# Four recurrent and attention layers on one core: x transposed once, the first norm on transposed tiles with a broadcast row, the residual copy from the same transposes

## The chip, the cores and the metric

The kernel runs on one core of a Trainium2 chip. Its engines work side by side, each on its own instruction queue in order: TensorE (PE, matmuls and transposes into PSUM; PEld is its weight load), VectorE (DVE), ScalarE (ACT), GpSimd (POOL) and SyncE (SP), whose queue issues the DMAs here. They wait for each other through semaphores. The metric is the device time of one execution in microseconds (us); for the kernel before, the median of three runs is 2333.66 us.

## The reference, cut to what matters

The input x has 1024 rows (positions) of 1024 channels, in f32. Two blocks of two layers each follow one another: a gated linear recurrence, attention with a shared low-rank cache, a layer with differential attention and a state-space scan, and sliding-window attention. Each layer adds its result to x. The change is in the first norm and the first lines of the first layer:

```python
def rms_norm(x, g):
    xf = x.astype(jnp.float32)
    y = xf * lax.rsqrt(jnp.mean(xf * xf, axis=-1, keepdims=True) + EPS)
    return (y * g.astype(jnp.float32)).astype(x.dtype)

def rglru_layer(x, norm_g, w_in, conv_w, ...):
    h = rms_norm(x, norm_g)
    u = h @ w_in
    xb, gate = u[..., :D_RNN], u[..., D_RNN:]
    xb = causal_depthwise_conv(xb, conv_w, conv_b)
    ...
    y = hs.astype(x.dtype) * jax.nn.silu(gate)
    return y @ w_out

x = x + rglru_layer(x, norm_a[layer], ...)
```

So every row of x needs one factor, the reciprocal root of its mean square, every channel one gain, and x itself is needed again for the residual.

## The kernel before, in words

Matmuls contract over the partitions, so activations are kept transposed: channels on the 128 partitions, positions along the free axis, in two halves of 512 positions. An f32 product is made of three matmuls in the fast format f32r: each operand is split into a rounded part and a remainder (`split`: ScalarE casts, VectorE subtracts), and high times high, high times low and low times high are added in PSUM (`mm3`, called by `proj`). The normalized input of a layer is the set of tiles `hT`: for each half, high and low, eight channel blocks in four tiles.

`start_phase` makes the first `hT`. It loads x in eight tiles `xt` of 128 positions, each in two halves, and the gains once for all 128 partitions (`gb`). For each tile ScalarE squares and sums the rows (into `xn`, whose content is not used), VectorE and POOL make the factor `r`, VectorE multiplies by factor and gain (`xn`), TensorE transposes (`tp0`, shown as `tp_140` and so on), and the result is split straight from PSUM. Then, with a lower priority (`LATE`), it transposes the raw `xt` again (`tpx`), copies to SBUF (`xe`, on ScalarE or VectorE, whichever is free) and stores to the DRAM scratch `xT_d`, from which the first layer's `out_proj` later reads the residual. `load_cols` loads small gains as rows, transposes them (`cps`) and keeps them as columns.

`layer_A` then projects with `w_in` in five pairs of 128 output channels. The weights come through `load_w`: loads `raw`, splits `whi` and `wlo`. In the first pair (`pr == 0`) the matmuls are 256 positions wide, so that they can begin when a quarter of x is ready; in the other pairs they are 512 wide. Each needs all eight channel blocks.

The order of the instructions on each engine is not the order of the code. Every call is recorded as an `Op` with a price in nanoseconds (`price`), its predecessors and its buffers, and `schedule` plays the whole program through in a list schedule: whenever an engine is free it takes the ready operation with the lowest priority number (its place in the code plus a bias). What comes out is emitted in `emit`, so all instructions carry line 429. A price that changes can therefore move instructions in every stage. Buffers come from pools with a limit for each name; a tile is given out when the plan finds one free. The stages after the start are, in order of time: the recurrence (to about 290 us), its output projection (to 390), the second layer's norm and projections, its attention, its output projection (to 935), the third layer, the fourth, and the last projection with the final norm.

Of the kernel before, what the change touches and what calls it, by code (L numbers as in the profile page):

```python
# [10 lines left out]
F32 = mybir.dt.float32  # L11
F32R = mybir.dt.float32r
AF = mybir.ActivationFunctionType
ALU = mybir.AluOpType
# [4 lines left out]
D = 1024  # L19
HALF = 512  # L20
# [153 lines left out]
class Program:  # L174
# [78 lines left out]
    def price(self, op):  # L253
# [40 lines left out]
    def schedule(self):  # L294
# [40 lines left out]
        while left:  # L335
            progress = False
            for e in engines:
# [95 lines left out]
def tile_kernel(ctx: ExitStack, tc: tile.TileContext, A, cc, out, stages="AMEO", dump=False):  # L433
# [38 lines left out]
    def begin(**tags):  # L472
        E.begin({k: v for k, v in tags.items()})
        E.cur.update(gtag)
# [62 lines left out]
    def split(hi, lo, src):  # L537
        splits((hi, lo, src))
# [168 lines left out]
    def start_phase(wsrc):  # L707
        begin(hT=("c4", 17), xt=("c4", 6), gb=("c4", 4), xn=("c4", 2), xe=("c2", 7), rows=("c2", 2), r1=("xs", 12),
              tp0=("ps", 2), tpx=("ps", 2), cps=("ps", 1))
        ht = new_hT()  # L710
        E.sync.dma_start(out=ident, in_=cc[:, C_ID:C_ID + 128])
        gb = T("gb", [128, D])
        xts, w = [], None
        for t in range(8):
            xt = T("xt", [128, D])
            for q in range(2):
                E.sync.dma_start(out=xt[:, q * 512:(q + 1) * 512], in_=A["x"][0, t * 128:(t + 1) * 128, q * 512:(q + 1) * 512])
            xts.append(xt)
            if t == 0:
                E.sync.dma_start(out=gb, in_=A["norm_a"][0].partition_broadcast(128))  # L720
            if t == WPOS:
                w = load_w(*wsrc)
        for t in range(8):
            xt, h, o = xts[t], t // 4, (t % 4) * 128
# [3 lines left out]
            E.vector.tensor_scalar(out=r[:, 1:2], in0=r[:, 0:1], scalar1=1.0 / D, scalar2=1e-6, op0=ALU.mult, op1=ALU.add)  # L728
            E.gpsimd.tensor_tensor(out=r[:, 2:3], in0=r[:, 1:2], in1=mhalf[:, 0:1], op=ALU.pow)
            for q in range(2):  # L730
                qs = slice(q * 512, (q + 1) * 512)
                E.vector.scalar_tensor_tensor(out=xn[:, qs], in0=xt[:, qs], scalar=r[:, 2:3], in1=gb[:, qs], op0=ALU.mult, op1=ALU.mult)
                tp = T("tp0", [128, 4, 128])
                for j in range(4):
                    E.tensor.transpose(tp[:, j], xn[:, (q * 4 + j) * 128:(q * 4 + j + 1) * 128], ident)
                splits(*[[ht[h][n][q * 2 + j][:, :, o:o + 128] for n in range(2)] + [tp[:, 2 * j:2 * j + 2]] for j in range(2)])
        E.bias += LATE
        for t in range(8):
            for q in range(2):
                tp = T("tpx", [128, 4, 128])  # L740
                for j in range(4):
                    E.tensor.transpose(tp[:, j], xts[t][:, (q * 4 + j) * 128:(q * 4 + j + 1) * 128], ident)
                xe = T("xe", [128, 4, 128])
                E.scalar.copy(xe, tp)
                E.alt("vector", "tensor_copy", (), dict(out=xe, in_=tp))
                E.sync.dma_start(out=xT_d[q * 4:(q + 1) * 4, :, t * 128:(t + 1) * 128].rearrange("k p s -> p k s"), in_=xe)
        E.bias -= LATE
        load_cols(0, [("norm_a", R(A["norm_a"][0])), ("conv_w", R2(A["conv_w"][0])), ("conv_b", R(A["conv_b"][0])),
                      ("b_rg", R(A["b_rg"][0])), ("b_ig", R(A["b_ig"][0])), ("lam", R(A["lru_lambda"][0])),
# [67 lines left out]
    def layer_A(ht, nxt):  # L817
# [14 lines left out]
        for pr in range(5):  # L832
# [12 lines left out]
            if pr == 0:  # L845
                for h in range(2):
                    pss = [T("mm", [128, HALF]) for b in range(2)]
                    for t in range(2):
                        ts = slice(t * 256, (t + 1) * 256)
                        for b in range(2):  # L850
                            proj(pss[b][:, ts], wx, b * 128, lambda k: tuple(x[k // 2][:, k % 2, ts] for x in ht[h]), 8)
                    for b in range(2):
                        E.scalar.copy(xss[b][:, 3 + h * HALF:3 + (h + 1) * HALF], pss[b])
# [688 lines left out]
```

## Time and profile before

| | |
|---|---|
| median of three runs | 2333.66 us (2333.2 to 2335.78) |
| the profiled execution: time, span | 2334.89 us, 2333.1 us |
| PE busy in the span | 2302.8 us (99%), 12233 instructions |
| PEld, DVE, ACT, POOL busy | 1943.9, 1575.0, 1273.2, 97.1 us |
| mean granted TensorE clock | 0.998 of full speed |
| DMA | 191.60 MB, 82 GB/s on the mean |

The span runs from the first to the last instruction. A busy time is the sum over an engine's instructions, overlaps taken once. A matmul's own duration holds its way through the array, so the pace of matmuls that follow one another is read from how many fit into a stretch, not from their mean. A wait is an idle time of an engine together with what ended it. The granted clock is the share of TensorE's full speed of 2.4 GHz that the chip allowed; 0.50 is its lower level, 1.2 GHz.

### The profile page before, as it was taken

How to read it: one execution, taken by the hardware profiler on the slowest of the kernel's cores; microseconds unless marked ns; L12 is line 12 of the kernel's file. 1: busy time of each engine (PE TensorE's matmuls, PEld its weight loads, DVE VectorE, ACT ScalarE, POOL GpSimd, SP SyncE). 2: the span in 40 equal slices, each digit the busy share in tenths (PEclk: the TensorE clock that was granted, in tenths of full speed). 3: DMA queues.
4: the chain of work that ended last, by engine and by line, in shares of the span. 5: the costliest groups of instructions: out<-in, count | busy, mean ns of one | idle time of the engine just before them, and what ended most of it. 6: DMA issues, size and time to landing. Idle time of an engine off the chain costs nothing.

```text
span 2333.1 us, 33127 instructions
## 1 busy us (share of the span) xinstructions
PE 2302.8 (99%) x12233; PEld 1943.9 (83%) x12233; DVE 1575.0 (68%) x3646; ACT 1273.2 (55%) x2653; POOL 97.1 (4%) x133
## 2 busy tenths in 40 slices
PE   8999999999999999999999999999999999999998
PEld 7888788778999888889898988888878888888877
DVE  6666735553777865876776758787776336787775
ACT  6766723332666653565656656585542125777751
POOL 0000001110000001000000000000001000000000
PEclk9999999999999999999999999999999999999999
DMA  6211322222112512312112111343243113111341
GB/s 191 84 41 37 113 95 90 73 84 82 48 55 60 194 55 67 109 42 59 38 44 58 44 55 48 106 121 116 69 176 138 55 55 108 50 55 46 112 141 73
DMA packets 171189, 191.60 MB, mean 82 GB/s; under 512 B 18294, under 2 KB 129170, under 8 KB 171026
## 3 DMA queue, kind: packets, MB, share of 16 engines
q1 hardware_dynamic: 171025, 189.48, 25.7%
q8 instruction: 96, 1.57, 0.3%
q14 instruction: 68, 0.55, 0.1%
HBM read 145.30 MB, written 42.04 MB: 80 GB/s over the span
## 4 chain that ended last, share of the span: by engine, by line
PE 96%; DVE 2%; ACT 1%; DMA 1%; issue 0%; SPq 0%; POOL 0%; DVEq 0%; POOLq 0%; ACTq 0%
PE mm L429 53%; PE ops L429 19%; PE sc L429 8%; PE ov L429 6%; PE tps L429 4%; PE yo L429 1%; PE tp L429 1%; PE mg L429 1%; PE nps L429 1%; PE aux L429 1%; DMA gb<-in_norm_a_dram 0%; PE ftp L429 0%; ACT s L429 0%; DVE xn L429 0%; PE tpx L429 0%
## 5 line engine op out<-in xcount | busy, mean ns | idle before, releaser
L429 PE MATMUL mm<-hT,whi 128*128 128x512 f32 (+1 forms) x3136 | 1002.9, 394 | 0.5 <-ACT whi L429 0.5
L429 PEld LDWEIGHTS mm<-hT,whi 128*128 128x128 f32 x3136 | 577.4, 188 | 120.9 <-issue 1.7
L429 PE MATMUL mm<-hT,wlo 128*128 128x512 f32 (+1 forms) x1568 | 616.2, 394 | 0.0
L429 PEld LDWEIGHTS mm<-hT,wlo 128*128 128x128 f32 x1568 | 294.8, 188 | 58.8 <-issue 0.5
L429 ACT ACTIVATE s<-s,st 128x257 f32<-128x257 f32 (+9 forms) x446 | 284.7, 656 | 92.9 <-DVE st L429 89.9
L429 DVE TENSOR_TENSOR wlo<-raw,whi 128x512 fp32r<-128x512 f32 (+4 forms) x316 | 200.4, 656 | 73.9 <-ACT whi L429 33.8
L429 ACT CAST whi<-raw 128x512 fp32r<-128x512 f32 (+4 forms) x316 | 176.1, 587 | 71.7 <-DVE wlo L429 44.9
L429 PE MATMUL ops<-yl,whi 128*128 128x512 f32 x544 | 214.3, 395 | 0.3 <-DVE yl L429 0.3
L429 PE MATMUL ops<-yh,whi 128*128 128x512 f32 x544 | 213.8, 395 | 0.0
L429 PE MATMUL ops<-yh,wlo 128*128 128x512 f32 x544 | 213.3, 394 | 0.0
L429 DVE TENSOR_TENSOR pl<-tps,ph 128x512 fp32r<-128x512 f32 (+2 forms) x284 | 142.9, 535 | 79.8 <-ACT ph L429 77.8
L429 DVE TENSOR_TENSOR xr<-ops,xr 128x512 f32<-128x512 f32 x96 | 65.9, 690 | 187.9 <-PE ops L429 187.9
L429 DVE CUSTOM_DVE_ANT_0 s<-sc,bt 128x256 f32<-128x256 f32 (+3 forms) x320 | 149.9, 491 | 36.5 <-PE sc L429 35.0
L429 ACT CAST ph<-tps 128x512 fp32r<-128x512 f32 (+2 forms) x284 | 121.3, 469 | 97.2 <-PE tps L429 95.4
L429 PE MATMUL ov<-ph,v 128*128 128x256 f32 (+2 forms) x700 | 159.6, 286 | 0.8 <-ACT ph L429 0.7
L429 ACT ACTIVATE sq<-xr 128x512 f32<-128x512 f32 x58 | 36.7, 632 | 208.7 <-DVE xr L429 208.6
L429 PE MATMUL tps<-ident,s 128*128 128x128 f32 x816 | 137.5, 273 | 0.2 <-DVE pl L429 0.2
L429 PEld LDWEIGHTS ov<-ph,v 128*128 128x128 f32 x700 | 118.1, 189 | 11.6 <-ACT ph L429 3.2
L429 PEld LDWEIGHTS ops<-yl,whi 128*128 128x128 f32 x544 | 102.1, 188 | 24.6 <-DVE yl L429 1.1
L429 PEld LDWEIGHTS ops<-yh,whi 128*128 128x128 f32 x544 | 102.0, 188 | 24.1 <-issue 0.3
L429 PEld LDWEIGHTS ops<-yh,wlo 128*128 128x128 f32 x544 | 102.2, 188 | 23.6
L429 PE MATMUL ov<-pl,v 128*128 128x256 f32 (+1 forms) x380 | 117.5, 309 | 0.5 <-DVE pl L429 0.5
(295 smaller groups left out, 3884.6 us busy)
## 6 DMA issues: line engine op xcount, KB each, us to landing
raw<-in_w_in_a_dram SPq DMA_DIRECT2D x72, 512.0 KB
raw<-in_w_out_a_dram SPq DMA_DIRECT2D x24, 512.0 KB
xr<-xT_d SPq DMA_DIRECT2D x24, 512.0 KB
yl<-yA_d SPq DMA_DIRECT2D x48, 256.0 KB
raw<-in_w_in_c_dram SPq DMA_DIRECT2D x18, 512.0 KB
xT_d<-xr SPq DMA_DIRECT2D x32, 256.0 KB
yA_d<-y SPq DMA_DIRECT2D x32, 256.0 KB
csb<-cs_d SPq DMA_DIRECT2D x16, 512.0 KB
```

The lines of the kernel that those rows point to most:

```text
L429: getattr(getattr(nc, op.eng), op.method)(*[conv(a) for a in op.args], **{k: conv(v) for k, v in op.kwargs.items()})
```

## The change

x is loaded in whole tiles of 128 positions. The gains come as a column (`cols["norm_a"]`, by an early `load_cols`) instead of a row spread over all partitions. For each half of 512 positions, four tiles are squared, the four columns of factors are made at once, spread on a diagonal (`dg`), and one plain f32 matmul with a matrix of ones puts the row of 512 factors on all partitions (`bc0`, in PSUM). Raw x is transposed once (`tp0`); `xe` is the copy in SBUF, one channel block by 512 positions. From `xe` VectorE makes `xn` with the gain column and the factor row, and `split` makes `hT`; the same `xe` is stored to `xT_d`. The `tpx` transposes and the bias `LATE` there are gone. In `layer_A` the first pair's matmuls are 512 wide and half by half. In `price` the matmul prices change, and in `schedule` the assumed DMA rate goes from 200 to 300 bytes per nanosecond.

```diff
         elif op.method == "matmul":
             fast = any(x.base.dt == F32R for x in reads)
             if fast:
-                op.cost = max(107, n / 2.4) + 2.5
+                op.cost = max(109, n * 0.449 + 2.5)
             elif n == 1:
-                op.cost = 150
+                op.cost = 224
             else:
-                op.cost = n / 0.6 * (0.55 if v.shape[0] == 64 else 1) + 2.5
+                op.cost = max(224, n / 0.6) * (0.5 if v.shape[0] == 64 else 1) + 2.5
...
-                    dma_free = max(dma_free, now + 2000) + op.nbytes / 200.0
+                    dma_free = max(dma_free, now + 2000) + op.nbytes / 300.0
...
     def start_phase(wsrc):
-        begin(hT=("c4", 17), xt=("c4", 6), gb=("c4", 4), xn=("c4", 2), xe=("c2", 7), rows=("c2", 2), r1=("xs", 12),
-              tp0=("ps", 2), tpx=("ps", 2), cps=("ps", 1))
+        begin(hT=("c4", 17), xt=("c4", 8), sqx=("c4", 2), xe=("c2", 7), xn=("c2", 3), rows=("c2", 2), dg=("c2", 1), r1=("xs", 12),
+              tp0=("ps", 3), bc0=("ps", 2), cps=("ps", 1))
...
+        load_cols(2, [("norm_a", R(A["norm_a"][0]))])
         xts, w = [], None
         for t in range(8):
             xt = T("xt", [128, D])
-            for q in range(2):
-                E.sync.dma_start(out=xt[:, q * 512:(q + 1) * 512], in_=A["x"][0, t * 128:(t + 1) * 128, q * 512:(q + 1) * 512])
+            E.sync.dma_start(out=xt, in_=A["x"][0, t * 128:(t + 1) * 128])
             xts.append(xt)
-            if t == 0:
-                E.sync.dma_start(out=gb, in_=A["norm_a"][0].partition_broadcast(128))
...
-        for t in range(8):
-            xt, h, o = xts[t], t // 4, (t % 4) * 128
-            r = T("r1", [128, 4])
-            xn = T("xn", [128, D])
-            E.scalar.activation(xn, xt, AF.Square, accum_out=r[:, 0:1])
...
-        E.bias += LATE
-        for t in range(8):
-            for q in range(2):
-                tp = T("tpx", [128, 4, 128])
...
+        gain = cols["norm_a"]
+        for h in range(2):
+            r = T("r1", [128, 8])
+            for j in range(4):
+                junk = T("sqx", [128, D])
+                E.scalar.activation(junk, xts[h * 4 + j], AF.Square, accum_out=r[:, j:j + 1])
+            E.vector.tensor_scalar(out=r[:, 0:4], in0=r[:, 0:4], scalar1=1.0 / D, scalar2=1e-6, op0=ALU.mult, op1=ALU.add)
+            E.gpsimd.tensor_tensor(out=r[:, 4:8], in0=r[:, 0:4], in1=mhalf[:, 0:4], op=ALU.pow)
+            dg = T("dg", [128, 4, 128])
+            E.vector.tensor_tensor(out=dg, in0=ident.unsqueeze(1).to_broadcast([128, 4, 128]),
+                                   in1=r[:, 4:8].unsqueeze(2).to_broadcast([128, 4, 128]), op=ALU.mult)
+            bc = T("bc0", [128, 512])
+            E.tensor.matmul(bc, lhsT=ones_r.bitcast(F32), rhs=dg.rearrange("p a b -> p (a b)"), start=True, stop=True)
+            for k in range(8):
                 tp = T("tp0", [128, 4, 128])
                 for j in range(4):
+                    E.tensor.transpose(tp[:, j], xts[h * 4 + j][:, k * 128:(k + 1) * 128], ident)
+                xe = T("xe", [128, 512])
+                E.scalar.copy(xe, tp.rearrange("p a b -> p (a b)"))
+                E.alt("vector", "tensor_copy", (), dict(out=xe, in_=tp.rearrange("p a b -> p (a b)")))
+                xn = T("xn", [128, 512])
+                E.vector.scalar_tensor_tensor(out=xn, in0=xe, scalar=gain[:, k:k + 1], in1=bc, op0=ALU.mult, op1=ALU.mult)
+                split(ht[h][0][k // 2][:, k % 2], ht[h][1][k // 2][:, k % 2], xn)
+                E.sync.dma_start(out=xT_d[k, :, hs(h)], in_=xe)
...
-            for b, h in ([] if pr == 0 else [(0, 0), (0, 1), (1, 0), (1, 1)]):
+            for b, h in ([(0, 0), (1, 0), (0, 1), (1, 1)] if pr == 0 else [(0, 0), (0, 1), (1, 0), (1, 1)]):
                 ps = T("mm", [128, HALF])
                 proj(ps, wx, b * 128, hrhs(ht, h), 8)
```

TensorE's queue before, from its first instruction on: `tpx` are transposes of raw x, `tp_140` and so on those of normalized x, `mm` the first projection.

```order
L429 MATMUL tpx<-ident,xt 128x128 x8
L429 MATMUL tp_140<-ident,xn 128x128 x4
L429 MATMUL tpx<-ident,xt 128x128 x3
L429 MATMUL tp_152<-ident,xn 128x128 x4
L429 MATMUL tpx<-ident,xt 128x128 x13
L429 MATMUL tp_215<-ident,xn 128x128 x4
L429 MATMUL tpx<-ident,xt 128x128 x3
L429 MATMUL tp_231<-ident,xn 128x128 x4
L429 MATMUL tpx<-ident,xt 128x128 x5
L429 MATMUL tp_257<-ident,xn 128x128 x4
L429 MATMUL tp_274<-ident,xn 128x128 x4
L429 MATMUL mm<-hT,whi 128x256 x4
```

And now, from the last transpose of the third channel block on, with the factor row `bc_217` and the first projection matmuls:

```order
L429 MATMUL tp_123<-ident,xt 128x128
L429 MATMUL tp_161<-ident,xt 128x128 x4
L429 MATMUL tp_168<-ident,xt 128x128 x4
L429 MATMUL tp_179<-ident,xt 128x128 x4
L429 MATMUL tp_188<-ident,xt 128x128 x4
L429 MATMUL tp_198<-ident,xt 128x128 x4
L429 MATMUL bc_217<-dg,ones_r 128x512
L429 MATMUL tp_223<-ident,xt 128x128
L429 MATMUL tp_225<-ident,xt 128x128
L429 MATMUL tp_223<-ident,xt 128x128
L429 MATMUL tp_225<-ident,xt 128x128
L429 MATMUL mm<-hT,whi 128x512 x2
```

The first projection matmul stood behind 24 transposes of four tiles of x and 32 of the copy; it now stands behind all 32 transposes of a half and the factor row, and the copy has no transposes of its own.

VectorE's queue now, from the first evacuation on (`r_115` the mean squares of four tiles, `cols_77` the gain column, `wlo` the weights' remainder):

```order
L429 COPY xe<-tp_117 128x512
L429 COPY xe<-tp_119 128x512
L429 TENSOR_SCALAR r_115<-r_115 128x4
L429 COPY xe<-tp_161 128x512
L429 COPY xe<-tp_168 128x512
L429 TENSOR_TENSOR wlo<-raw,whi 128x512 x2
L429 TENSOR_TENSOR dg<-ident,r_115 128x512
L429 TENSOR_TENSOR wlo<-raw,whi 128x512 x2
L429 SCALAR_TENSOR_TENSOR xn<-xe,cols_77,bc_217 128x512 x3
L429 TENSOR_TENSOR hT<-xn,hT 128x512
L429 SCALAR_TENSOR_TENSOR xn<-xe,cols_77,bc_217 128x512
L429 TENSOR_TENSOR hT<-xn,hT 128x512 x2
```

Before, the first `xn` was VectorE's third instruction after one evacuation; now four evacuations and four weight remainders stand ahead of it.

SP's queue of DMAs now, in the middle of the start (`rows` are the small gains, `raw` the next weights):

```order
L429 DMA rows<-in_conv_b_a_dram 12x128
L429 DMA xT_d<-xe 128x512 x7
L429 DMA rows<-in_ssd_norm_a_dram 8x128
L429 DMA rows<-in_subln_a_dram 1x128
L429 DMA rows<-in_norm_c_dram 8x128
L429 DMA rows<-in_b_in_c_dram 18x128
L429 DMA raw<-in_w_in_a_dram 128x4x256 x2
L429 DMA xT_d<-xe 128x512 x7
```

Seven stores of the copy have moved ahead of the last four gain loads and of the next weights; before, the first store was issued behind all gain loads.

## Rows read from the trace of the kernel before

**Rows 1.** The page's line of TensorE: busy us, share of the span, instructions.
```profile
PE 2302.8 (99%) x12233; PEld 1943.9 (83%) x12233; DVE 1575.0 (68%) x3646; ACT 1273.2 (55%) x2653; POOL 97.1 (4%) x133
```

**Rows 2.** Busy us by stretch: length, PE, PEld, DVE, ACT, POOL, PEclk, DMA share, GB/s.
```profile
0.00:60.00 60.00, 48.44 (x344) 45.39 (x345) 41.12 (x102) 37.22 (x81) 4.89 (x16) 0.97 0.64 194
60.00:2230.00 2170.00, 2161.19 (x11486) 1824.11 (x11485) 1473.50 (x3430) 1201.64 (x2494) 87.79 (x109) 1.00 0.25 79
2230.00:2333.10 103.10, 93.17 (x406) 74.35 (x405) 60.42 (x116) 34.30 (x80) 4.41 (x8) 0.98 0.20 72
```

**Rows 3.** TensorE's waits, first stretch and middle: us in total, times, longest.
```profile
PE tpx L429 <- DMA xt<-in_x_dram: 4.0, 1, 4.0
...
PE nps L429 <- ACT dh L429: 3.3, 3, 1.6
PE mm L429 <- ACT krh L429: 2.1, 2, 1.4
...
PE ov L429 <- DVE pl L429: 0.5, 1, 0.5
```

**Rows 4.** The chain that ended last, from the start: start us, us, what.
```profile
2.12 7.06 DMA gb<-in_norm_a_dram
...
11.95 0.85 PE tp L429 x4
...
39.03 0.44 PE tp L429 x4
...
42.73 8.05 PE mm L429 x68
...
65.70 3.72 PE mm L429 x16
```

**Rows 5.** Timeline of TensorE at plain f32 products: start us, us, what.
```profile
1516.57 1.72 PE L429 MATMUL tp<-xdd,BN 128*128 128x128 f32 x14
1518.05 0.48 PE L429 MATMUL mm<-hT,whi 128*128 128x512 f32 x1
```

**Rows 6.** Busy us of short stretches at the start, columns as in rows 2.
```profile
4.00:7.00 3.00, 1.94 (x8) 1.57 (x8) 0.85 (x2) 1.63 (x3) 0.00 (x0) 1.00 0.82 182
9.00:13.00 4.00, 2.78 (x13) 2.81 (x14) 2.17 (x4) 0.65 (x2) 0.00 (x0) 1.00 1.07 385
14.84:16.95 2.11, 0.01 (x1) 0.00 (x1) 1.44 (x5) 2.11 (x6) 0.55 (x1) 1.00 0.84 298
17.40:20.80 3.40, 3.40 (x18) 3.33 (x16) 2.45 (x8) 2.20 (x6) 0.55 (x1) 0.50 0.58 186
```

**Rows 7.** Groups by form: busy us, mean ns | idle before.
```profile
L429 ACT ACTIVATE xn<-xt 128x1024 f32<-128x1024 f32 x8 | 8.6, 1074 | 0.0
...
L429 DVE COPY xe<-tpx 128x512 f32<-128x512 f32 x2 | 1.4, 692 | 6.1 <-PE tpx L429 6.1
...
L429 POOL TENSOR_TENSOR r<-r,mhalf 128x4 f32<-128x4 f32 x32 | 37.0, 1158 | 817.3 <-DVE r L429 804.8 <-DMA yB_d<-yb 6.3 <-DVE sk L429 3.4
...
L429 DVE TENSOR_TENSOR wlo<-raw,whi 128x512 fp32r<-128x512 f32 x8 | 5.1, 682 | 0.0
...
L429 DVE SCALAR_TENSOR_TENSOR xn<-xr,cols,nps 128x512 f32<-128x512 f32 x16 | 11.2, 741 | 0.4 <-PE nps L429 0.4
```

**Rows 8.** Timeline, pairs that follow at once: start us, us of both, what.
```profile
9.32 1.41 DVE L429 SCALAR_TENSOR_TENSOR xn<-xt,r,gb 128x512 f32<-128x512 f32 x2 [2.34 <-DMA gb<-in_norm_a_dram]
...
391.04 1.28 DVE L429 TENSOR_TENSOR hT<-xn,hT 128x512 fp32r<-128x512 f32 x2
...
389.96 1.22 ACT L429 CAST hT<-xn 128x512 fp32r<-128x512 f32 x2 [2.58 <-DVE xn L429]
```

**Rows 9.** The `tpx` tiles' TensorE instructions after the last 256-column matmul.
```profile
50.73:66.00 15.27, 6.78 (x32) 1.00 0.72 206
```

**Rows 10.** Timeline of SP's queue: the first stores of the copy.
```profile
25.25 4.44 SPq L429 DMA_DIRECT2D xT_d<-xe  x6
```

**Rows 11.** The page's group of the remainders of transposed attention tiles.
```profile
L429 DVE TENSOR_TENSOR pl<-tps,ph 128x512 fp32r<-128x512 f32 (+2 forms) x284 | 142.9, 535 | 79.8 <-ACT ph L429 77.8
```

More of the change, by code (lines that the diff above doesn't have):

```diff
@@ L707, in start_phase @@
     def start_phase(wsrc):
-        begin(hT=("c4", 17), xt=("c4", 6), gb=("c4", 4), xn=("c4", 2), xe=("c2", 7), rows=("c2", 2), r1=("xs", 12),
-              tp0=("ps", 2), tpx=("ps", 2), cps=("ps", 1))
+        begin(hT=("c4", 17), xt=("c4", 8), sqx=("c4", 2), xe=("c2", 7), xn=("c2", 3), rows=("c2", 2), dg=("c2", 1), r1=("xs", 12),
+              tp0=("ps", 3), bc0=("ps", 2), cps=("ps", 1))
         ht = new_hT()
         E.sync.dma_start(out=ident, in_=cc[:, C_ID:C_ID + 128])
-        gb = T("gb", [128, D])
+        load_cols(2, [("norm_a", R(A["norm_a"][0]))])
         xts, w = [], None
@@ L715, in start_phase @@
             xt = T("xt", [128, D])
-            for q in range(2):
-                E.sync.dma_start(out=xt[:, q * 512:(q + 1) * 512], in_=A["x"][0, t * 128:(t + 1) * 128, q * 512:(q + 1) * 512])
+            E.sync.dma_start(out=xt, in_=A["x"][0, t * 128:(t + 1) * 128])
             xts.append(xt)
-            if t == 0:
-                E.sync.dma_start(out=gb, in_=A["norm_a"][0].partition_broadcast(128))
             if t == WPOS:
                 w = load_w(*wsrc)
-        for t in range(8):
-            xt, h, o = xts[t], t // 4, (t % 4) * 128
-            r = T("r1", [128, 4])
-            xn = T("xn", [128, D])
-            E.scalar.activation(xn, xt, AF.Square, accum_out=r[:, 0:1])
-            E.vector.tensor_scalar(out=r[:, 1:2], in0=r[:, 0:1], scalar1=1.0 / D, scalar2=1e-6, op0=ALU.mult, op1=ALU.add)
-            E.gpsimd.tensor_tensor(out=r[:, 2:3], in0=r[:, 1:2], in1=mhalf[:, 0:1], op=ALU.pow)
-            for q in range(2):
-                qs = slice(q * 512, (q + 1) * 512)
-                E.vector.scalar_tensor_tensor(out=xn[:, qs], in0=xt[:, qs], scalar=r[:, 2:3], in1=gb[:, qs], op0=ALU.mult, op1=ALU.mult)
+        gain = cols["norm_a"]
@@ L733, in start_phase @@
                 tp = T("tp0", [128, 4, 128])
                 for j in range(4):
-                    E.tensor.transpose(tp[:, j], xn[:, (q * 4 + j) * 128:(q * 4 + j + 1) * 128], ident)
-                splits(*[[ht[h][n][q * 2 + j][:, :, o:o + 128] for n in range(2)] + [tp[:, 2 * j:2 * j + 2]] for j in range(2)])
-        E.bias += LATE
-        for t in range(8):
-            for q in range(2):
-                tp = T("tpx", [128, 4, 128])
[L741 to L746, printed above, removed]
@@ L747, in start_phase @@
-        E.bias -= LATE
-        load_cols(0, [("norm_a", R(A["norm_a"][0])), ("conv_w", R2(A["conv_w"][0])), ("conv_b", R(A["conv_b"][0])),
+                    E.tensor.transpose(tp[:, j], xts[h * 4 + j][:, k * 128:(k + 1) * 128], ident)
[4 more added lines that the diff above has]
+                E.vector.scalar_tensor_tensor(out=xn, in0=xe, scalar=gain[:, k:k + 1], in1=bc, op0=ALU.mult, op1=ALU.mult)
@@ L749, in start_phase @@
+                split(ht[h][0][k // 2][:, k % 2], ht[h][1][k // 2][:, k % 2], xn)
+                E.sync.dma_start(out=xT_d[k, :, hs(h)], in_=xe)
+        load_cols(0, [("conv_w", R2(A["conv_w"][0])), ("conv_b", R(A["conv_b"][0])),
                       ("b_rg", R(A["b_rg"][0])), ("b_ig", R(A["b_ig"][0])), ("lam", R(A["lru_lambda"][0])),
@@ L844, in layer_A @@
                 xss.append(xs)
[L845 to L853, printed above, removed]
-            for b, h in ([] if pr == 0 else [(0, 0), (0, 1), (1, 0), (1, 1)]):
+            for b, h in ([(0, 0), (1, 0), (0, 1), (1, 1)] if pr == 0 else [(0, 0), (0, 1), (1, 0), (1, 1)]):
                 ps = T("mm", [128, HALF])
```

## The prediction

> **What bounds the kernel now.** I read the page first: TensorE is busy 2302.8 us, 99% of the span, so the kernel can only gain by less TensorE work or fewer TensorE waits [rows 1]. Then the busy time by stretch. Idle is the length minus PE busy: 60.00 - 48.44 = 11.56 us in the first 60 us, 2170.00 - 2161.19 = 8.81 us in the long middle, and 103.10 - 93.17 = 9.93 us in the last stretch, whose tail the change does not touch [rows 2]. Then TensorE's waits: the first thing it waits for is x, 4.0 us; in the middle the largest wait is for the norms' `dh`, 3.3 us [rows 3]. Last the start's chain in order of time. It runs through the load of `gb` until 9.18 us, then TensorE takes over, and its pitches are to be seen there: four transposes in 0.85 us early on (0.21 each) and in 0.44 us later (0.11 each), 68 projection matmuls of 256 columns in 8.05 us (0.118 each), 16 of 512 columns in 3.72 us (0.2325 each) [rows 4].
>
> **TensorE work.** Before, x is transposed twice: 64 tiles `tp0` of normalized x and 64 tiles `tpx` of raw x. After, 64 in all, so 64 x 0.11 = 7.0 us go. The first projection was 192 matmuls of 256 columns, 192 x 0.118 = 22.7 us, and becomes 96 of 512, 96 x 0.2325 = 22.3. Two new matmuls copy the row of 512 factors to all partitions (`bc0`). They are plain f32, which the trace does not show at 512 columns. Its nearest row is the plain product `tp<-xdd,BN`: 14 records, that is 7 products of 128 columns, in 1.48 us until the next matmul, 0.21 each, so 4 x 0.21 = 0.85 us for 512 columns [rows 5]. The bounds are 0.23 (as if it went like a split matmul) and 1.7 (at the lower clock); I take 0.85 by that row. Work falls by 7.0 + 0.4 - 1.7 = 5.7 us.
>
> **When the projection can start.** Before, each 128-row tile of x was normalized by itself, and the projection began on halves of the columns. After, four tiles must have been loaded and squared before one factor row exists. I walk this path.
> Loads: half of the first tile is usable at 4.0 us, where TensorE's wait for it ends [rows 3]. At 9 to 13 us, when only x and weights were in flight, 385 GB/s moved; at 4 to 7 us, with `gb` among them, 182 [rows 6]. `gb` (one 4 KB row read 128 times) is gone, so I take 385: 0.524 MB per tile is 1.36 us. With the second half (0.7) and a short load ahead of it (0.2), tile 1 is there at 4.9, tile 4 at about 9.1, the weights' halves at 10.5 and 11.8, the other x tiles by 17.3. At 182 GB/s tile 4 would come at 13.5, which is the upper bound.
> Chain: the Square of tile 4 takes 1.07 us and its sum is read by 10.4 [rows 7]. VectorE, in order, still has two `xe` copies of 0.69 to do, which wait for the fourth tile's transposes at the early pitch; the mean is done at 11.3, and POOL's power of four columns (1.16) at 12.5 [rows 7]. VectorE is then still in two more copies and two `wlo` (0.68 each), so the diagonal `dg` runs 13.9 to 14.5, the `bc0` matmul to 15.5, two more `wlo` hold VectorE until 16.2, the first `xn` (0.74) ends at 16.95, ScalarE's cast (0.62) at 17.7, and with 0.3 of hand-over the first matmul starts at 18.0 [rows 7, 8].
>
> **From there on.** For each 128 channels VectorE now has one `xn` and one remainder. In pairs these take 0.67 (1.41 for two less 0.74) and 0.60 (1.28 less 0.68), 1.27 together; TensorE has 6 x 0.2325 = 1.395 of matmuls for them [rows 4, 7, 8]. So TensorE stays the slower one, by little. To the first half's end it has 48 x 0.2325 = 11.2, 32 transposes of the second half (3.5), the second `bc0` (0.85), 0.2 of small transposes, and by the order about 0.6 of waits for the first remainders: 18.0 + 16.3 = 34.3. The second factor row is ready at 30.0, so TensorE's own queue hides it by 4.3 us; if that cover went, the second half would wait for VectorE as the first does. The second half adds 11.2 and about 0.4 of waits for channels 6 and 7: 45.9 us.
> Before, the last matmul of 256 columns ends at 42.73 + 8.05 = 50.78 [rows 4], and 32 of the `tpx` transposes come after it, as the stretch's own count shows [rows 9]: 32 x 0.11 = 3.5, so the same point is at 54.3. Gain 54.3 - 45.9 = 8.4 us. The copy's 16 evacuations to SBUF are as many as before, beside TensorE's work.
>
> **SP's queue.** The copy's 16 stores move forward. Six of them were issued from 25.25 us on [rows 10]; now seven stand ahead of the last four small gain loads and of the next weights. Behind those loads TensorE has the transposes of the gains (`cps`) in its queue, just before the end of the first half, and behind that the second factor row. With the stores issued from about 19.6 to 21.4 us, the last gain load is issued at 23.8 and lands by 26; TensorE comes there at 28. So 2 us of cover, and if the loads took longer, each us would stop TensorE for one. The next weights, issued behind them near 25 and landed near 30, are wanted at 46.
>
> **The clock.** Before, TensorE did almost nothing from 14.84 to 16.95, and from 17.4 to 20.8 the granted clock was 0.50, the lower level [rows 6]. After, it has only `bc0` to do between about 14 and 18, so I expect a stretch at 0.50 there again, now under the first matmuls instead of under transposes. The cost is 0 (all inside waits for VectorE) to 3.4 / 2 + 0.85 = 2.55 us; I take the middle, 1.2.
>
> **The rest of the program.** The instruction order of the whole program comes from a list scheduler, and four of its prices change, so every later stage is reordered too: nothing is added there, but waits can move. They are 8.81 us in all now, which bounds a gain; the loss is bounded in rival three at 14.2. The new prices are the truer ones (0.2325 measured for 512 columns; 512 x 0.449 + 2.5 = 232 ns priced, 216 before). That favours neither sign: planned cover then equals real cover, so some reserve that TensorE's lateness gave is lost. I take +0.9.
> The Trainium skill, page TensorE: Matmul & The Clock Gate, section Back-to-back issue gap, gives columns / 2.4 + 2.5 ns, 216 ns for 512 columns, which is just the old price. The trace differs (0.2325) and decides; by the page's figure the new prices would be the wrong ones, TensorE would run 7% ahead of its plan, and rival three would gain weight, while the start's 96 matmuls would be 1.6 us shorter.
>
> **Sum.** -8.4 + 1.2 + 0.9 = -6.3 us on the profiled execution's 2334.89 us (span 2333.1 and 1.8 around it), so 2328.6. The median of the runs shown, 2333.66, lies 1.23 below that execution: 2327.4.
>
> **Rivals.** One: x is slow by itself, not through `gb`. For it: 4 to 7 us is also the first burst of all. Against it: the 4 us after it, same queue, same source, run at twice the rate. At 182 GB/s the first matmul comes 4.5 us later: 2331.9.
> Two: the truer prices remove the middle's hand-over waits. For it: the largest, `nps<-dh` 3.3 and `krh` 2.1 us, are places where the plan put too few matmuls [rows 3]. Against it: at both there is little other work to put. Without these 5.4 and without my +0.9: 2321.1.
> Three, the slower side: the lost reserve. Where TensorE waits for a split of a transposed tile (284 `ph`, `pl` pairs, [rows 11]), about three matmuls lie between as cover, each priced 0.0167 us more now, so the plan covers 0.05 us less. If all 284 turned that into a wait: 14.2 us, and 2327.4 - 0.9 + 14.2 = 2340.7. It decides from 0.042 us per pair on. Against it: only 0.5 us of waits for `pl` stand in the middle now, and a wait once taken moves the rest along with it.
>
> **How the numbers follow.** A measurement of this kernel tells 0.2%, 4.7 us, from no change: faster means under 2329.0, slower over 2338.3. Forecast 0.55 (its own range 2324 to 2331, three quarters of it under 2329.0), rival one 0.22, rival two 0.15, rival three 0.08. Faster: 0.41 from the forecast, 0.15 from rival two, 0.04 from rival one's near edge, 0.60. Slower: 0.07 of rival three. The same: 0.33. The range runs from just below rival two, 2320, past rival one to 2335, which leaves out rival three and the far ends of the bounds.
>
> **What would show it.** TensorE's matmul records fewer by about 160 at the start (64 transposes, 96 halves) and its PE busy lower by some 5 us; no wait for `gb`; the first `mm` near 18 us and the last of the first projection near 46; a stretch at 0.50 clock near 17 to 21; idle of the middle still near 9 us. The forecast is wrong if the first `mm` comes after 22 us, if VectorE's pair takes over 1.4 us per 128 channels so that TensorE waits at each, or if the middle's idle goes beyond 15 us.

## The result and the profile after

The changed kernel takes 2352.77 us (median of six runs) and the kernel before 2335.31 beside it. The ratio is 1.0075, 95% interval 1.0062 to 1.0088: slower by 17.5 us, where 6.3 us faster was forecast. The profiled execution took 2350.48 us, span 2348.7 (before 2333.1). Both profiled executions have a mean granted clock of 0.998, so the 15.6 us between their spans do not come from the clock.

TensorE's line of the page, which answers to [rows 1]:

```profile
PE 2310.1 (98%) x12078; PEld 1926.8 (82%) x12078; DVE 1578.7 (67%) x3646; ACT 1258.1 (54%) x2618; POOL 98.0 (4%) x127
```

There are 155 matmuls fewer, as forecast, and yet TensorE is busy 7.3 us longer. The stretches, columns as in [rows 2]:

```profile
0.00:60.00 60.00, 48.27 (x213) 38.18 (x214) 43.95 (x89) 39.68 (x68) 2.56 (x11) 0.97 0.62 218
60.00:2230.00 2170.00, 2153.45 (x11378) 1801.66 (x11377) 1459.76 (x3399) 1174.07 (x2450) 90.91 (x107) 1.00 0.24 76
2230.00:2348.70 118.70, 108.39 (x491) 86.94 (x489) 75.02 (x159) 44.36 (x102) 4.53 (x9) 0.98 0.30 107
```

The middle's idle time went from 8.81 to 16.55 us. That is past the 15 us which the prediction named as its refutation, but these 7.7 us are only half of the loss. The same 2170 us hold 108 matmuls fewer (x11378, x11486 in [rows 2]), and part of a late matmul's delay stands in the trace as busy time: the product at 1157.69 us, shown further down, starts 0.47 us later than the pace allows, and only 0.30 of it is idle. TensorE's waits of 60 to 2300 us, which answer to [rows 3]:

```profile
PE ops L429 <- DVE yl L429: 3.2, 2, 2.3
PE tp L429 <- DVE xsil L429: 2.7, 1, 2.7
PE mm L429 <- ACT krh L429: 2.4, 2, 1.7
PE nps L429 <- ACT dh L429: 2.1, 3, 1.1
PE ov L429 <- ACT ph L429: 1.9, 6, 0.5
```

`nps<-dh` became shorter. The wait for `xsil`, and one of 1.1 us for `wlo` further down the list, are new. All six waits for `ph` lie in the attention stages; before there was one, near the end:

```profile
PE ov L429 <- ACT ph L429: 0.7, 1, 0.7
```

**How the loss is measured.** For every two matmuls that follow one another I take the time from start to start, less the pace of the first one's shape (the median of the trace: 232.4 ns for 512 columns, 174 for 384, 125 for 272, 117.5 for 256, 109 for 128 and less; the same in both kernels). The sum of what is left is the *excess*. I split it by time: start (0 to 100 us), *repeated stages* (500 to 900, 1000 to 1500, 1900 to 2200 us: the three attention stages, which repeat a pattern for every few heads), and *stage changes* (all the rest).

| us | start | repeated stages | stage changes | all |
|---|---|---|---|---|
| before | 13.4 | 3.0 | 14.1 | 30.4 |
| after | 16.0 | 16.4 | 21.0 | 53.4 |

Excess rose by 23.0 us and the work at pace fell by 6.1 (2291.2 to 2285.1), +16.9 for a span that grew by 15.6. At equal work still to do, the changed kernel is 4.7 us ahead at 60 us, 3.5 ahead at 400, 0.9 behind at 900, 6.2 at 1500, 9.3 at 1800 and 15.7 at 2200. So the start won something, and then the program lost time nearly everywhere.

**The clock inside the excess.** Excess also holds what the granted clock costs. To see how much, I count for each matmul half of the time that it spent at 0.50, but no more than its excess; this is an estimate from the trace. It is 1.7 us of the start before and 1.5 after. Between 100 and 2300 us neither profiled execution has a stretch at 0.50, so the rise of the repeated stages (13.4 us) and of the stage changes (6.9) does not come from the clock. For the stage changes the lists of TensorE's waits show most of it: against before, `hT` and `yl` wait 1.1 us more each, `dl` 0.9, `xsil` 2.7 where `xdd` had 1.1, `wlo` and `whi` 1.1 and 0.7 where there was none, and `dh` 1.8 less.

**The start.** The first matmul came at 17.78 us (walked: 18.0). The end of the first projection is 49.40, where the 97th `mm` starts; the prediction had 45.9 without the clock. Why it came late stands in the chain of the changed kernel (start us, us, what):

```profile
19.95 2.04 DMA xT_d<-xe
...
22.01 0.75 DVE xn L429
22.75 0.61 DVE hT L429
...
23.41 0.50 PE mm L429
```

The fourth `xn` was given a buffer that a copy tile `xe` had held, and waited until that copy's store had landed: VectorE stood 3.01 us, TensorE 2.71. After this wait the clock fell; windows with the columns of [rows 2], the granted clock third from the end:

```profile
22.00:23.40 1.40, 0.00 (x0) 0.00 (x0) 1.39 (x3) 0.61 (x2) 0.00 (x0) 1.00 1.00 382
23.40:25.00 1.60, 1.59 (x6) 1.41 (x7) 1.60 (x3) 1.41 (x4) 0.00 (x0) 0.66 0.99 376
25.00:26.00 1.00, 1.00 (x4) 0.73 (x3) 1.00 (x3) 0.85 (x3) 0.00 (x0) 0.50 0.64 246
26.00:27.00 1.00, 1.00 (x4) 0.81 (x3) 1.00 (x2) 0.96 (x2) 0.00 (x0) 0.50 0.12 32
27.40:28.00 0.60, 0.60 (x5) 0.42 (x4) 0.60 (x2) 0.60 (x2) 0.00 (x0) 1.00 0.99 341
```

From 24.08 to 27.21 seven 512-column matmuls took 3.13 us instead of 7 x 0.2325 = 1.63, so this stretch at the lower level of 1.2 GHz cost 1.5 us.

### The profile page after: what moved, and what is told of

Its sections match the earlier page's. It is cut to its first block, busy times and chain, and to the rows that moved or that the text cites. A ratio compares the mean times of both kernels' runs of the same rounds, so it can differ in the third digit from the quotient of the medians.

```text
span 2348.7 us, 32769 instructions
## 1 busy us (share of the span) xinstructions
PE 2310.1 (98%) x12078; PEld 1926.8 (82%) x12078; DVE 1578.7 (67%) x3646; ACT 1258.1 (54%) x2618; POOL 98.0 (4%) x127
## 4 chain that ended last, share of the span: by engine, by line
PE 86%; DVE 7%; ACT 3%; DMA 1%; issue 1%; POOL 0%; SPq 0%; DVEq 0%; POOLq 0%; ACTq 0%
PE mm L429 47%; PE ops L429 18%; PE sc L429 7%; PE ov L429 5%; PE tps L429 4%; DVE s L429 2%; PE yo L429 2%; PE mg L429 1%; PE tp L429 1%; PE nps L429 1%; ACT kd L429 1%; DVE xn L429 1%; ACT s L429 1%; PE aux L429 1%; DVE hT L429 0%
## 5 line engine op out<-in xcount | busy, mean ns | idle before, releaser
L429 PE MATMUL mm<-hT,whi 128*128 128x512 f32 x3072 | 1001.1, 399 | 4.2 <-DVE hT L429 3.0
L429 PEld LDWEIGHTS mm<-hT,whi 128*128 128x128 f32 x3072 | 570.4, 188 | 125.7 <-DVE hT L429 3.7
L429 PE MATMUL mm<-hT,wlo 128*128 128x512 f32 x1536 | 610.8, 399 | 1.1 <-DVE wlo L429 1.1
L429 PEld LDWEIGHTS mm<-hT,wlo 128*128 128x128 f32 x1536 | 289.3, 188 | 63.2 <-DVE wlo L429 1.7
L429 ACT ACTIVATE s<-s,st 128x257 f32<-128x257 f32 (+9 forms) x429 | 271.4, 649 | 121.3 <-DVE st L429 119.0
```

Of the source, the lines that this page charges most:

```text
L429: getattr(getattr(nc, op.eng), op.method)(*[conv(a) for a in op.args], **{k: conv(v) for k, v in op.kwargs.items()})
```

## The experiments

All times are ratios to the kernel before, run beside them. The first four separate the new start from the new prices.

**e_old_prices**: the changed kernel with all prices and the DMA rate of before (the price hunks of the diff undone).

> The changed kernel with the four prices and the DMA rate of before: the new start alone. Prices at fault (the plan's order for the middle is what costs): the middle's hand-overs are as before, and what is left is the start, which ends its first projection at 49.4 us instead of 54.3: 2335.3 - 4.9 = 2330 us, 2326 to 2334, middle's idle near 9 us. Start at fault (its buffers or its finish spoil what follows): near 2352 as the changed kernel. Lottery (every new order of the middle loses some, because another start also reorders it): 2336 to 2350.

**e_new_prices**: the kernel before with the price hunks alone.

> The kernel before with the four new prices and the new DMA rate: the new order alone, the start's code as before. Prices at fault: 2335.3 plus the 17.5 lost and the 4.9 that the start had gained, about 2357 us (2350 to 2362). Start at fault: 2335, within 3. Lottery: 2337 to 2355, which by itself does not tell it from the prices.

**e_fast216**: one price put back in the changed kernel:
```diff
-                op.cost = max(109, n * 0.449 + 2.5)
+                op.cost = max(107, n / 2.4) + 2.5
```


> The changed kernel with one price put back: the 512-column split matmul at 215.8 ns (now 232.4), all else new. Lost reserve (the matmul's truer price takes away cover): nearly all of the loss goes, 2328 to 2334 us. The DMA rate or the small products' prices at fault: 2348 to 2353. Lottery: anywhere from 2335 to 2353.

**e_dma200**: only the DMA rate put back:
```diff
-                    dma_free = max(dma_free, now + 2000) + op.nbytes / 300.0
+                    dma_free = max(dma_free, now + 2000) + op.nbytes / 200.0
```


> The changed kernel with only the DMA rate put back to 200 bytes per ns, all prices of matmuls new. Lost reserve: no gain, 2348 to 2356 us. DMA rate at fault (loads planned too early or stores too dense): 2328 to 2336. Lottery: anywhere from 2335 to 2360.

Measured: 2335.14 us (0.9995, interval 0.9986 to 1.0003), 2356.89 (1.0089, 1.0076 to 1.0103), 2333.88 (0.9995, 0.9986 to 1.0004) and 2359.88 (1.0103, 1.0089 to 1.0117). So the prices cost the time, whichever start stands ahead of them; and of the prices, that of the split matmuls does it (the edit sets it for all widths; it is named here by its 512-column value). The repeated stages' excess was 3.6, 16.5, 3.7 and 15.2 us. The DMA rate of before made it worse by some 6.5 us, and e_dma200 lies past the 2348 to 2356 that lost reserve gave it; in its profiled execution 7.9 us of excess are at a clock of 0.50, where the changed kernel has 1.5. e_old_prices missed too: it should have kept its start's gain of 4 us, but no gain can be told from the measurement. Its lead of 4.0 us at 60 us shrank by 1.5 at 85 us (new waits for `wlo`, 0.6, and `whi`, 0.4), 1.1 at 406 (a wait of 1.4 for `dh` where before has 0.3) and 1.5 at 947. The last of these is the clock alone: the waits for `dh`, `dl` and `hT` just ahead are the same in both traces (0.44, 0.27, 1.31 and 0.15 or 0.16 us), but the clock is not. From 944 to 947 us, columns as in [rows 2], before:

```profile
944.00:947.00 3.00, 3.00 (x22) 2.90 (x23) 3.00 (x6) 1.16 (x2) 0.00 (x0) 1.00 0.02 5
```

e_old_prices:

```profile
944.00:947.00 3.00, 3.00 (x15) 2.99 (x14) 3.00 (x5) 1.86 (x3) 0.00 (x0) 0.50 0.00 0
```

The next three ask whether it goes by amount, and whether the missing cover can be asked for in another way.

**e_fast224** and **e_fast200**: the same price at 224.1 and at 200 ns (`n * 0.4329 + 2.5`, `n * 0.3857 + 2.5`).

> The changed kernel with the 512-column split matmul priced halfway, 224.1 ns (215.8 gave 2333.9, 232.4 gave 2352.8). Lost cover, by the amount: about halfway, 2339 to 2348 us. A threshold at some tile's due time: at one of the ends. Lottery: off the line between them, either way.

> The changed kernel with the 512-column split matmul priced at 200 ns, well under what it takes. Lost cover: a deeper reserve, so not slower than with 215.8 ns, and little left to win: 2326 to 2334 us. Lottery, or a plan that pays for too much cover elsewhere (tiles held longer, buffers late): 2337 to 2355.

**e_cover150**: true prices, longer hand-overs in the plan:
```diff
-        "scalar": dict(tensor=270, ...
+        "scalar": dict(tensor=420, ...
-        "vector": dict(tensor=256, ...
+        "vector": dict(tensor=406, ...
```


> The changed kernel, all its prices kept true; instead the plan reckons 150 ns more for each hand-over from ScalarE and from VectorE to TensorE (270 to 420, 256 to 406). Lost cover (a plan with true prices puts just as many matmuls between a tile's producer and its consumer as the bare latency needs, so each delay shows): the cover is asked for in another coin and most of the 18 us come back, 2330 to 2340 us, the middle's excess pitch back near that of before. Pace (it is the price as such, by the times at which the plan sets loads and the other engines' work): no gain, 2346 to 2360. Lottery: anything from 2335 to 2360.

**e_fast216_xn**: e_fast216 with buffers of their own for the start's `xn`:
```diff
-... xe=("c2", 7), xn=("c2", 3), ...
+... xe=("c2", 7), xn=("c4", 4), ...
```


> The changed kernel with the 512-column price at 215.8 ns and the normalized tiles of the start in four buffers of the 4-KB class of their own, so that the fourth does not wait until a stored copy has left its buffer (3.0 us on VectorE, 2.7 of it on TensorE). If the start's time reaches the end: 2333.9 - 2.7 = 2331 us, first projection done by 46.8 us. If later stages swallow it, as they seem to swallow part of the 4.9 us: 2333 to 2336, with the projection done early all the same.

Measured: e_fast224 2340.43 us (1.0026, 1.0015 to 1.0037), e_fast200 2332.23 (0.9991, 0.9982 to 1.0000), e_cover150 2346.30 (1.0053, 1.0041 to 1.0066), e_fast216_xn 2337.90 (1.0016, 1.0007 to 1.0025). The first two are as a lost reserve has it. e_cover150 brought back a third of the loss and not most of it (repeated stages 13.0 us), and its total lies in the range of the rival, the price as such. So longer hand-overs do not stand in for the lower price. e_fast216_xn missed both cases: the wait at 22 us is gone, but the first projection ended at 50.31. Its VectorE timeline (start us, us, what, the idle time before and its releaser) shows where the wait went:

```profile
34.39 0.69 DVE L429 TENSOR_TENSOR gl<-gr,gh 128x512 fp32r<-128x512 f32 x1 [5.18 <-DMA xT_d<-xe]
```

A split of the gates' weights, in the same class of buffers, now waits for a store of the copy, and `xn` is queued behind it on VectorE.

**What happens in a repeated stage.** ScalarE before and after at the same place of the third layer (four casts `kd`, then the high half `ph` of a transposed score tile). Before:

```profile
1151.13 2.35 ACT L429 CAST kd<-mm 64x512 fp32r<-64x512 f32 x4
1153.50 0.62 ACT L429 CAST whi<-raw 128x512 fp32r<-128x512 f32 x1
1154.23 0.62 ACT L429 CAST kl<-kl 64x512 fp32r<-64x512 f32 x1
1154.87 0.59 ACT L429 CAST ph<-tps 128x512 fp32r<-128x512 f32 x1
```

After:

```profile
1153.51 2.35 ACT L429 CAST kd<-mm 64x512 fp32r<-64x512 f32 x4
1155.89 1.14 ACT L429 CAST whi<-raw 128x512 fp32r<-128x512 f32 x2
1157.05 0.58 ACT L429 CAST ph<-tps 128x512 fp32r<-128x512 f32 x1
```

And TensorE between the tile's transposes and the product that uses `ph`, before:

```profile
1154.10 0.49 PE L429 MATMUL tps<-ident,s 128*128 128x128 f32 x3
1154.34 0.47 PE L429 MATMUL mm<-hT,wlo 128*128 128x512 f32 x1
1154.66 0.63 PE L429 MATMUL mm<-hT,whi 128*128 128x512 f32 x2
1155.12 0.39 PE L429 MATMUL mm<-hT,wlo 128*128 128x512 f32 x1
1155.36 0.63 PE L429 MATMUL mm<-hT,whi 128*128 128x512 f32 x2
1155.82 0.28 PE L429 MATMUL ov<-ph,v 128*128 128x256 f32 x1
```

After:

```profile
1155.75 0.49 PE L429 MATMUL tps<-ident,s 128*128 128x128 f32 x3
1155.99 0.48 PE L429 MATMUL mm<-hT,whi 128*128 128x512 f32 x1
1156.31 0.39 PE L429 MATMUL mm<-hT,wlo 128*128 128x512 f32 x1
1156.54 0.62 PE L429 MATMUL mm<-hT,whi 128*128 128x512 f32 x2
1156.99 0.40 PE L429 MATMUL mm<-hT,wlo 128*128 128x512 f32 x1
1157.69 0.39 PE L429 MATMUL ov<-ph,v 128*128 128x256 f32 x1 [0.30 <-ACT ph L429]
```

Two things moved. The plan put five matmuls in place of six between transposes and product. And `ph` begins 1.30 us after the transposes began (1155.75 to 1157.05) instead of 0.77 (1154.10 to 1154.87), because ScalarE runs later against TensorE: `kd` began 2.97 us ahead of the transposes (1151.13, 1154.10) and now only 2.24 (1153.51, 1155.75), and as before two more casts stand between `kd` and `ph`. The product starts 0.47 us later than the pace allows. The same happens at 1291.74 and 1425.80, once in each period of 134.1 us. The period holds all of its waits, not this one alone: the median distance of `v<-mm` casts 16 apart is 132.68 us before and 134.04 after.

The plan thinks that those casts fit. It prices a 512-column cast at 480 to 520 ns where the trace has 587 to 618, and VectorE's differences at 602 where it has 687. With TensorE's price alone made true, the plan's TensorE is slower against a ScalarE that is still too fast; that this is why ScalarE comes late is so far an argument. The next four test this by *ratio of prices*.

**e_true_act**, **e_true_dve**, **e_true_all**: the changed kernel with true prices also on ScalarE, on VectorE, on both; **e_true_216**: both, and the matmul at 215.8.
```diff
-            op.cost = 53 + n * 0.834 + (40 if sb else 0)
+            op.cost = 158 + n * 0.834 + (40 if sb else 0)
...
-                op.cost = 69 + n * 1.041
+                op.cost = 154 + n * 1.041
...
```
Left out are the same change of VectorE's base for its other operations, its corrections for tiny and accumulating ones (-40 and +82 ns), and ScalarE's accumulated sum (93 to 195 ns).

> The changed kernel with ScalarE's prices alone made true as well. Ratio of prices: ScalarE casts the high halves that open most waits, and is the engine priced lowest (480 against 587), so most of the loss goes, 2330 to 2342 us. TensorE's price by itself: 2346 to 2358.

> The changed kernel with VectorE's prices alone made true as well. Ratio of prices: part of the loss goes, less than with ScalarE's, 2336 to 2348 us. TensorE's price by itself: 2346 to 2358.

> The changed kernel with its true TensorE prices, and now ScalarE's and VectorE's prices as the trace has them too: base 53 to 158 ns on ScalarE (a 512-column cast was priced 480 and takes 587), its accumulated sum 93 to 195, base 69 to 154 on VectorE (a 512-column difference was priced 602 and takes 687). Ratio of prices (all three engines were priced some 7 to 20% too low, so with TensorE alone made true the plan queues more work on ScalarE ahead of a tile that TensorE needs than fits): the loss goes, 2326 to 2336 us. TensorE's price by itself (the pace at which the plan runs TensorE): 2346 to 2358.

> The changed kernel with ScalarE's and VectorE's prices as the trace has them and the 512-column matmul at 215.8 ns, 7% under what it takes: true prices and reserve together. Ratio of prices and reserve both right: the best of all, 2324 to 2333 us. If too much cover costs elsewhere: 2334 to 2345.

Measured: e_true_act 2346.08 us (1.0045, 1.0033 to 1.0057), e_true_dve 2340.44 (1.0024, 1.0015 to 1.0032), e_true_all 2346.73 (1.0045, 1.0033 to 1.0057), e_true_216 2352.13 (1.0085, 1.0066 to 1.0103). By the total the ratio theory missed on three of the four: e_true_act and e_true_all lie in the range of its rival, and e_true_216 was the opposite of what it said. By parts it is half right. In e_true_act a single cast stands between `kd` and `ph` at the same place, `ph` even waits for its transposes, and TensorE's timeline shows no wait for it:

```profile
1157.43 2.36 ACT L429 CAST kd<-mm 64x512 fp32r<-64x512 f32 x4
1159.82 0.63 ACT L429 CAST whi<-raw 128x512 fp32r<-128x512 f32 x1
1160.66 0.59 ACT L429 CAST ph<-tps 128x512 fp32r<-128x512 f32 x1 [0.21 <-PE tps L429]
```

The repeated stages fell from 16.4 to 8.6 (ScalarE), 5.4 (VectorE) and 4.1 us (both). What e_true_all lost instead is at the stage changes, 31.5 us. Its largest single wait there is in the stretch 1500 to 1700 us, where the list of the kernel before has none:

```profile
PE mm L433 <- DVE wlo L433: 5.1, 1, 5.1
```

During this wait the clock fell:

```profile
1570.00:1576.00 6.00, 5.16 (x12) 4.09 (x13) 6.00 (x7) 4.26 (x9) 0.28 (x2) 0.50 0.59 141
```

Such stretches make up 11.2 of the 31.5 us, so without them the stage changes are at 20.3, near the 21.0 of the changed kernel. They are no accident of one execution: the five runs of e_true_all have a mean granted clock of 0.993 to 0.996, those of the kernel before beside them 0.996 to 0.999. Without the clock's part the whole excess is 28.7 us before, 51.9 after, 44.2 in e_true_act, 36.2 in e_true_dve, 35.3 in e_true_all and 44.9 in e_true_216. So true prices on VectorE, alone or with ScalarE's, took back some 16 of the 23 us, ScalarE's alone a third, against the order that the theory had expected, and the clock then hid much of it.

In e_true_216 the third layer alone has 10.6 us of repeated excess, 1.5 of it at a clock of 0.50; TensorE waits there 3.4 us for `pl`, in four waits of up to 0.9.

The last six ask whether the differences at the stage changes are chance, and try for a faster version. **e_shift233** and **e_shift217** add 1 ns to every split matmul's price (232.4 and 215.8 before). **e_fast208** and **e_fast190** fill the row. **e_fast200_xn** has the extra buffers of e_fast216_xn, **e_fast200_dma385** plans DMA at 385 bytes per ns.

> The changed kernel with every split matmul priced 1 ns dearer (512 columns at 233.4 ns), a change with no sense of its own. Two parts, price and chance: the excess pitch of the repeated stages (500 to 900, 1000 to 1500, 1900 to 2200 us) stays at 14 to 19 us, as it was 16.4; that of the stage changes (the other stretches after 100 us, 21.0 now) moves by several us either way; time 2347 to 2359. Price alone: both stay within 1.5 us, 2351 to 2355. Chance alone: the repeated stages move as much as the stage changes, 2335 to 2360.

> The same shift of 1 ns on the version priced at 215.8 ns (now 216.8). Price and chance: repeated stages 3 to 6 us (3.7 before), stage changes anywhere from 14 to 25 (21.8 before), time 2328 to 2339. Price alone: 2333 to 2336. Chance alone: 2330 to 2355 with the repeated stages anywhere.

> The changed kernel with the 512-column price at 208 ns. Price and chance: repeated stages 2 to 4 us, between those at 200 (2.1) and 215.8 (3.7); stage changes 14 to 25; time 2327 to 2338. Chance alone: no order in the repeated stages.

> The changed kernel with the 512-column price at 190 ns. Price and chance: repeated stages stay at 2 to 4 us, since nothing is left there to win, and the stage changes decide: 2328 to 2340 us. If ever more cover kept paying: under 2328. If too much of it costs (tiles are held longer): over 2340.

> The version priced at 200 ns, with four 4-KB buffers of their own for the normalized tiles of the start; a try for a version that beats both. First projection done by 47.1 us or before, repeated stages near 2; 2327 to 2334 us by price and chance, of which the stage changes (17.4 now) decide most. If the extra buffers move the plan as they did at 215.8, 2334 to 2340.

> The version priced at 200 ns with loads planned at 385 bytes per ns, the rate that the first loads showed, instead of 300. Price and chance: repeated stages near 2, time 2328 to 2340 us, a second draw of the stage changes and of the start. If the DMA rate has a cost of its own (200 instead of 300 cost 7 us in the changed kernel): a few us faster than 2332, 2324 to 2331.

| version | priced ns, 512 columns | ratio (interval) | repeated stages us | stage changes us | of these at clock 0.50 | period us |
|---|---|---|---|---|---|---|
| e_fast190 | 190 | 1.0008 (0.9999, 1.0016) | 2.0 | 22.3 | 3.1 | 132.71 |
| e_fast200 | 200 | 0.9991 (0.9982, 1.0000) | 2.1 | 17.4 | 1.5 | 132.58 |
| e_fast208 | 208 | 1.0000 (0.9992, 1.0009) | 3.3 | 18.0 | 3.1 | 132.63 |
| e_fast216 | 215.8 | 0.9995 (0.9986, 1.0004) | 3.7 | 21.8 | 6.3 | 132.84 |
| e_shift217 | 216.8 | 1.0007 (0.9998, 1.0016) | 3.4 | 18.3 | 3.1 | 132.68 |
| e_fast224 | 224.1 | 1.0026 (1.0015, 1.0037) | 10.1 | 20.3 | 3.1 | 133.61 |
| after | 232.4 | 1.0075 (1.0062, 1.0088) | 16.4 | 21.0 | 0 | 134.04 |
| e_shift233 | 233.4 | 1.0104 (1.0090, 1.0117) | 21.9 | 24.4 | 3.2 | 135.49 |

The repeated stages follow the price: flat up to 216.8 (2.0 to 3.7 us), then steep. The weight loader's waits for `ph` between 1100 and 1500 us (us in total, times) tell the same: none at 200 and 208 ns. Before, with 215.8 ns:

```profile
  PEld ov L429: 0.9, 4
```

e_fast224:

```profile
  PEld ov L429: 3.2, 9
```

After:

```profile
  PEld ov L429: 5.8, 18
```

e_shift233:

```profile
  PEld ov L429: 10.4, 28
```

The stage changes by themselves keep to no order, 17.4 to 24.4, and 1 ns moved them by +3.4 and by -3.5 us. That looks like chance in the plan, but it is the clock. In the profiled execution of e_shift233 it fell twice in these stages, where the changed kernel has no fall:

```profile
475.50:478.50 3.00, 3.00 (x8) 2.32 (x8) 3.00 (x7) 1.86 (x3) 0.56 (x1) 0.50 0.02 5
2257.50:2260.50 3.00, 3.00 (x13) 2.61 (x12) 2.53 (x6) 2.38 (x8) 0.00 (x0) 0.50 0.04 16
```

In that of e_fast216 it fell four times, in that of e_shift217 twice. e_fast216:

```profile
460.50:463.50 3.00, 3.00 (x8) 2.35 (x8) 1.81 (x3) 0.62 (x1) 0.00 (x0) 0.50 0.00 0
942.00:944.50 2.50, 2.50 (x11) 2.31 (x11) 2.50 (x5) 0.66 (x2) 0.00 (x0) 0.50 0.00 0
1522.00:1525.00 3.00, 3.00 (x8) 2.30 (x7) 3.00 (x9) 0.11 (x1) 0.00 (x0) 0.50 1.13 245
2239.00:2241.50 2.50, 2.50 (x11) 2.21 (x10) 2.23 (x5) 2.25 (x7) 0.00 (x0) 0.50 0.00 0
```

By the estimate each of these falls cost 1.5 to 1.6 us. Without them the stage changes are 14.9 to 15.9 us from 200 to 216.8 ns, 17.2 at 224.1, 21.0 and 21.2 at the top (19.2 at 190), and the two shifts of 1 ns moved them by +0.2 and -0.3. So above 216.8 ns the stage changes rise with the price too, and both parts of the loss follow it. How often the clock falls differs between executions of one kernel: e_fast216's profiled execution took 2338.61 us where the median of its eleven is 2333.88, and the kernel before averages 2332.8 us over the four of its 109 runs beside the experiments whose mean granted clock is 1.000, and 2338.7 over the two at 0.996. One expectation missed in the other direction: at 233.4 ns the repeated stages rose to 21.9, beyond the 14 to 19 forecast, 5.5 us for 1 ns; why so much is not shown. e_fast200_xn took 0.9995 (0.9986 to 1.0003) and ended its first projection at 50.46 us, not by the 47.1 expected, so the extra buffers failed a second time. e_fast200_dma385 took 1.0015 (1.0006 to 1.0024), inside its range. No version is clearly faster than the kernel before; the nearest is e_fast200.

## Why the prediction was wrong

**The rest of the program** is the step that failed. It was taken at +0.9 us and was +20.3 in the profiled executions (from 4.7 ahead at 60 us to 15.6 later at the end). By excess, 13.4 of it lie in the repeated stages and 6.9 at the stage changes, none of it at the lower clock, and e_fast216 takes back the loss by the split matmuls' price alone. Three points of its working failed:
- "That favours neither sign." The sign was negative, and there was a hint of it: one price was made true while those of ScalarE and VectorE stayed some 18 and 12% too low ([rows 7] has 682 ns for a difference that the plan prices at 602). That this ratio is what counts is only in part shown: true prices on VectorE took back some 16 of the 23 us of excess, once the clock's part is set aside, and ScalarE's less than 8.
- "A wait once taken moves the rest along with it." The order is the same in each period, and the same wait returned: about 0.47 us at 1023.59, 1157.69, 1291.74 and 1425.80 us.
- The bound of 14.2 us in rival three. Its mechanism, lost reserve, was the nearest of all, but its price took split pairs alone and 0.05 us each. The waits are fewer and larger, 0.2 to 0.5 us, the transposes of `s` wait too, and the stage changes were not in it. The range ended at 2335, below rival three, on a chance of 0.08; the measured 2352.77 lies past rival three's 2340.7 too.

**The start** had the right mechanism and its size was off: -8.4 and +1.2 for the clock were forecast, -7.2, and it was 4.7 us ahead at 60 us. Right were the first matmul (18.0, measured 17.78) and `bc0` (0.85; 0.86 for the second one). `xe` buffers freed only by their store were not walked: 2.71 us. The clock did fall once, with 1.5 us lost against 1.2 taken, but at 24 to 27 us, after a wait that was not foreseen, and not at 17 to 21: that the size came near is luck.

**TensorE work**: 5.7 us less was forecast, 6.1 measured at pace. But busy time rose by 7.3 us, so the test by busy time, which the prediction offered, did not show it.

**Rival one** did not come: 396 GB/s moved from 10 to 14 us. **Rival two** did not come either: `nps<-dh` and `krh` are 4.5 us of waits where they were 5.4.

**The Trainium skill's** figure of 216 ns for 512 columns (TensorE: Matmul & The Clock Gate, section Back-to-back issue gap) is given there for a matmul by itself. The pace here, where each matmul has its weight load, is 232.4 ns in both kernels. As a price in the plan the old 215.8 ns is the better one all the same, by 0.8% in e_fast216. The prediction named the reserve that TensorE's lateness against its plan gave, and put 0.9 us on its loss.

**What stays open.** Why a price above 217 ns costs so much was followed wait by wait at one place of the third layer alone; for the stage changes there are only the lists of waits. Which waits let the clock fall, and why it falls in some executions and not in others, was not tested. What good plans share may be the ratio of the matmul's price to ScalarE's (512-column cast from PSUM): 0.40 to 0.45 for all versions with repeated excess under 5 us (e_true_all 0.40), 0.47 and more at 10 us and over, 0.37 in e_true_216 at 11.6. Changing one partner's price alone breaks that row (e_true_dve has 0.48 with 5.4 us, e_true_act 0.40 with 8.6), and it was not put to a test of its own. Within 0.2% the new start is worth nothing that can be told apart: e_old_prices and e_fast216 equal the kernel before, though in the profiled executions, less the clock's part by the estimate (4.6 and 7.9 us, before 1.7), both are some 2.5 us ahead of it.

## What to carry to other kernels

In a list-scheduled kernel a price moves instructions in every stage. Making one engine's price true while its partners stay too cheap can cost more than the wrong price did, and price edits are to be timed apart from the edit that they come with. Here TensorE, busy 99% of the span, did better while it ran late against its plan; a wait of a fraction of a us inside a repeated pattern is multiplied by the repeats, and part of it hides in busy time, so look at the period of the pattern. Before a difference between two profiled executions is called chance or put down to the plan, look at the granted clock in the stretches where they differ. A tile that a store reads holds its buffer until the store lands, so whatever shares its pool waits for the DMA.

## What was not expected of the hardware

One wait of 2.71 us on TensorE at 21 to 23 us was followed by some 3 us at a granted clock of 0.50, that is 1.2 GHz: this wait cost half as much again (1.5 us). Later waits could have the same sequel and did not always: in e_fast216 a wait of 1.96 us for `krh`, ended at 459.92, was followed by a clock of 0.50 from 460.5 to 463.5; in the kernel before waits of 1.43 and 1.57 us ended at 463.42 and 467.58, and the clock stayed at 1.00 (460 to 471 us). A store of 0.26 MB that the plan counts at about 2.9 us (2 us and 300 bytes per ns, with nothing queued ahead) was in the chain for 2.04 us at 19.95 us, but the chain of e_fast216_xn holds one from 27.61 for 6.71 us, while 353 GB/s moved (30 to 36 us).
